# A hybrid encoder layer on one core: convolution bias on VectorE, group-norm statistics per pass, another order of the last four output pieces

## The chip, the cores and the metric

The kernel runs on one core of one Trainium2 chip. A core has a matrix engine (TensorE, PE in the profile; PEld is its weight load), VectorE (DVE), ScalarE (ACT), GpSimd (POOL) and SyncE (SP), which here issues every DMA. Matrix products land in PSUM, everything else lies in SBUF. The metric is the device time of one execution in microseconds. Of the kernel before there are three timed runs: 1142.69 us in the middle, 1141.70 and 1143.29 at the ends. The profile comes from one more execution, of 1140.08 us.

## What is computed

One layer with batch 1, 1024 positions and width 1024. Its first half mixes tokens: a normalised and modulated input goes through one projection, whose columns are split between a convolution group (512 channels) and an HGRN2 group of four heads; both results go through one output projection. The second half is an MLP of width 4096 with a squared ReLU. All in float32. The part that the change touches, cut down:

```python
def _conv_mixer(u_val, u_gate, w_dw, b_dw, gn_gain, gn_bias):
    u = u_val * jax.nn.sigmoid(u_gate)
    y = causal_depthwise_conv(u, w_dw) + b_dw          # 31 taps, 512 channels
    yf = y.reshape(B, S, CONV_GROUPS, CONV_CH // CONV_GROUPS)   # 8 groups of 64 channels
    mu = jnp.mean(yf, axis=-1, keepdims=True)
    var = jnp.mean(jnp.square(yf - mu), axis=-1, keepdims=True)
    yf = ((yf - mu) * lax.rsqrt(var + GN_EPS)).reshape(B, S, CONV_CH)
    return jax.nn.silu(yf * gn_gain + gn_bias)
```

`u_val` and `u_gate` come from the combined projection. Mean and variance are taken at each position over the 64 channels of a group.

## The kernel before

Matrix products are made with float32 operands split into a high and a low part: three matmuls for each product. ACT makes the high part, and DVE or POOL the low part (`split`, `halve`); which of the two is decided when the program is built.

The order of all instructions on all engines is fixed when the program is built. The class `Weave` keeps an estimated time for each engine and a list of side streams (Python generators). The main stream issues the big matmuls; at each of its steps the side streams whose due time has come issue their next piece. A changed cost, or a stream added at another moment, therefore moves instructions of other streams too. On the chip each engine takes its instructions strictly in that order and waits where an operand isn't there.

Stages, with their times on the profile's clock: the first three projections (to 73 us); gate, value and V columns (G, U, V, to about 257); the convolution between the last V columns and the following projections (232 to 296); the remaining projections `pj` beside the four HGRN2 heads (to 378); the output projection `pout` (to about 510); the MLP's up part `pup` (to 823); its down part, which alternates between the PSUM tiles `al` and `be` (to 1132).

**Convolution.** The gated input `u` is written to a DRAM buffer `udram`, and read back as `wide`, so that a window of 64 rows, 32 of a block of positions and 32 of the block before, lies in 64 partitions. `toep` holds Toeplitz matrices of the taps: a window's row times this matrix gives 32 outputs of one channel. The 512 channels go in two passes `p`, each with two rounds `q` of 64 channels times two partition halves `r`. Each pass loads `toep` (4 tiles), then `wide` by four DMAs, two for each half `r`. Row 0 of each window meets no tap (31 taps over 32 outputs leave it unused), so the host put the bias `b_dw` in row 0 of the Toeplitz matrices, and two more DMAs (line 710) overwrite row 0 of each half of `wide` with ones. SP issues such a DMA only when the load of the same half has landed, and what stands behind it in SP's order waits too.

The matmuls of a round write the PSUM tile `cv` (one buffer). `conv_evac` copies it on ACT into four result tiles `ys[s]`, 256 positions each, by 8 copies of 128 elements a round; the copies scatter (a step of 128 elements in the destination). When the last round of the second pass is copied, four streams `conv_norm(s)` start: DVE takes the mean over 64 channels for 16 groups (`gmu`, 128x16), subtracts it, ACT squares the whole tile, DVE sums the squares (`gvar`), POOL raises to the power -1/2 (`gr`), DVE multiplies. Then PE transposes the tile (`cpb`), ACT applies gain and bias, and a sigmoid and a product follow; the result is one operand of the output projection.

**Heads.** Each head takes q and f from projections `pj`. A matmul with ones (`pd`) and seven levels of small matmuls (`pl`, with block size h = 1 to 64) build its attention. Each level is a chain: `pl` on PE needs the q and k that DVE scaled for the level before.

**Last pieces.** The last down product `p4` has four output pieces `al[0]` to `al[3]` (128x512). `al[0]` and `al[1]` are halves of one PSUM tile, `al[2]` and `al[3]` of another. For the last three groups of the sum the main stream takes piece after piece, 18 matmuls each. After each piece a stream `last(n)` reads it on ACT (squares) and DVE (product with the gate), makes the norm's factor on POOL, adds to the residual on DVE and stores. A matmul that writes a PSUM tile waits until the readers of that tile are done.

Of the kernel before, what the change touches and what calls it, by code (L numbers as in the profile page):

```python
# [7 lines left out]
F32 = mybir.dt.float32  # L8
# [3 lines left out]
AF = mybir.ActivationFunctionType  # L12
ALU = mybir.AluOpType
AX = mybir.AxisListType

P = 128
# [34 lines left out]
EARLY, LATE = (4, 5, 0, 1, 2, 3), (6, 7)  # L51
FINAL = (0, 1, 3, 2, 5, 6, 4, 7)
# [155 lines left out]
class Weave:  # L208
# [30 lines left out]
    def after(self, key, extra=None):  # L239
        return max(self.t[key], self.now) + (EXTRA if extra is None else extra)  # L240
# [47 lines left out]
def block_kernel(ctx: ExitStack, tc: tile.TileContext, x, vecs, masks, rows, vrow, crow, wada_t, wada_n,  # L288
                 win0, win, wint, toep, wout, wup, wdn, out):
# [25 lines left out]
    def tiny(name, cols=1):  # L315
        if cols > 8:
            return small.tile([P, 16], F32, tag="tiny16", name=name, bufs=8)[:, 0:cols]
        return small.tile([P, 8], F32, tag="tiny", name=name, bufs=16)[:, 0:cols]
# [342 lines left out]
    S.dma_start(crow_s.f, crow.broadcast_to([P, 1024]))  # L661
    sig = [None] * 4
# [34 lines left out]
    def conv_input():  # L697
        yield slots.gone
        w = slots.wide().rearrange("p (b c) -> p b c", c=P)
        for p in range(2):  # L700
            yield room(4)
            toeps = [new() for _ in range(4)]
            for c in range(4):
                S.dma_start(toeps[c].f, toep[p, c])
            for r in range(2):
                nc.sync.dma_start(w[64 * r:64 * r + CB, :, :], udram[2 * p + r, :, 0:NB, :])
                nc.sync.dma_start(w[64 * r + CB:64 * r + 64, :, :], udram[2 * p + r, :, 1:NB + 1, :])
                wv.spend("S", 5.0)
            for r in range(2):
                nc.sync.dma_start(w[64 * r:64 * r + 1, :, :], ones[0:CB, :])  # L710
            yield wv.t["S"] + 2 * DLAT
            yield from conv_mm(p, w, toeps)
        slots.end_wide()
# [22 lines left out]
    def conv_evac(p, q, ps):  # L736
        pv = ps.rearrange("p (r i b) -> p r i b", r=2, i=16)
        for s in range(4):
            if ys[s] is None:
                yield room(1)  # L740
                ys[s] = new()
            yv = ys[s].f.rearrange("t (b p r q i) -> t p q r i b", p=2, r=2, q=2, i=16)
            for r in range(2):
                A.activation(yv[:, p, q, r], pv[:, r, :, 8 * s:8 * s + 8], AF.Copy)
        acc.done(ps, "A")
        yield after("A")
        if p and q:
            for s in range(4):
                wv.add(conv_norm(s), RNORM)

    def conv_norm(s):

        y = ys[s]
        yield after("A")
        yv = y.f.rearrange("p (a c) -> p a c", c=64)
        mu = tiny("gmu", 16)
        V.reduce_sum(mu, yv, axis=AX.X)
        V.tensor_scalar(mu, mu, 1.0 / 64, None, ALU.mult)
        V.tensor_tensor(yv, yv, mu[:, :, None].broadcast_to([P, 16, 64]), ALU.subtract)
# [3 lines left out]
        A.activation(sz.f, y.f, AF.Square)  # L763
        yield after("A")
        var = tiny("gvar", 16)
        V.reduce_sum(var, sz.f.rearrange("p (a c) -> p a c", c=64), axis=AX.X)
        r = rstd_of(var, 16, 1.0 / 64, 1e-5, "gr")
        yield after("G")
        V.tensor_tensor(yv, yv, r[:, :, None].broadcast_to([P, 16, 64]), ALU.mult)
        yield after("V")  # L770
# [985 lines left out]
    def down():  # L1756
# [32 lines left out]
        for n in range(4):  # L1789
            yield from down_mm("p4", al, False, range(NG - LASTG, NG), (n,))  # L1790
            wv.add(last(n, al[n]), -1)
# [89 lines left out]
def host_arrays(np, i):  # L1881
# [9 lines left out]
    for h in MASKED:  # L1891
# [18 lines left out]
    taps[0] = f("b_dw")[0]  # L1910
# [6 lines left out]
                win0=win0, win=win, wint=wint, toep=toep, wout=wo, wup=wup, wdn=wdn)  # L1917
# [18 lines left out]
```

## Time and profile before

| | us |
|---|---|
| median of three timed runs | 1142.69 (1141.70 to 1143.29) |
| the profiled execution | 1140.08 |
| its span, first to last instruction | 1138.3 |
| mean granted TensorE clock (share of full speed) | 0.979 |
| POOL busy | 282.2 |
| matmuls | 7036 |

A line of a timeline gives the start, the duration, engine, source line, operation, output and inputs, shapes and the number of instructions merged; in brackets stands how long the engine had been idle and what ended that. A line of a table of stretches gives busy time and number of instructions for PE, PEld, DVE, ACT and POOL in turn, then the granted clock, the share of the DMA engines and GB/s. A line of a group gives count, total busy time and mean in ns, then idle time before it. L235 is the helper that records the instructions of DVE, ACT, POOL and most DMAs, L1820 that of the matmuls, L413 the power of a norm. `s` stands for any of the 53 large SBUF tiles.

### The profile page before, as it was taken

Reading aid. Unit: us, or ns where it says so; the run is one execution under the profiler, and the core shown is the slowest. Engines: PE = TensorE matmul, PEld = TensorE weight load, DVE = VectorE, ACT = ScalarE, POOL = GpSimd, SP = SyncE. Lnnn points to the kernel's source line nnn. Section 1 sums busy time; section 2 is a strip of 40 time slices with the busy share of each in tenths; the row PEclk is TensorE's granted clock in tenths of the full one; section 3 lists DMA queues with packets and bytes.
Section 4 is the critical chain, followed back from the end, with each engine's and each line's share of the span. In section 5 each row is a group of like instructions: output and inputs, shape, how many; then the busy total and the mean of one; then the engine's idle time right before and its main releaser. Section 6 shows DMA issues by size and latency. Waiting matters only on the chain.

```text
span 1138.3 us, 17072 instructions
## 1 busy us (share of the span) xinstructions
PE 1089.6 (96%) x7036; PEld 886.2 (78%) x7036; DVE 708.1 (62%) x727; ACT 471.1 (41%) x687; POOL 282.2 (25%) x190
## 2 busy tenths in 40 slices
PE   6999989889999799989999999999999999999996
PEld 2787778768878688767888888888888888888885
DVE  3537667234588962665766975333266969997942
ACT  6731301014356423567452243556543334454530
POOL 5121131001193400482101420124400002304301
PEclk8999999989999799989999999999999999999999
DMA  9523434756021202374569745325667957674901
GB/s 365 198 73 127 147 105 136 198 165 176 23 75 56 94 2 56 113 261 169 197 244 324 290 166 194 112 56 170 218 237 268 326 203 245 217 278 153 336 11 74
DMA packets 57149, 195.21 MB, mean 171 GB/s; under 512 B 6256, under 2 KB 10736, under 8 KB 56816
## 3 DMA queue, kind: packets, MB, share of 16 engines
q1 hardware_dynamic: 57072, 194.13, 49.6%
q8 instruction: 55, 0.90, 0.3%
q14 instruction: 22, 0.18, 0.0%
HBM read 158.32 MB, written 35.72 MB: 170 GB/s over the span
## 4 chain that ended last, share of the span: by engine, by line
PE 78%; DVE 8%; DMA 7%; issue 2%; POOL 2%; ACT 2%; SPq 1%; DVEq 0%; POOLq 0%; ACTq 0%
PE pup L1820 26%; PE al L1820 15%; PE be L1820 11%; PE pout L1820 8%; DVE s L235 7%; PE pj L1820 6%; PE pf L1820 3%; DMA s<-in_wada_n 2%; PE ptV L1820 2%; POOL s L235 1%; ACT s L235 1%; PE po L1820 1%; PE cv L1820 1%; DMA wide<-udram 1%; PE pt L1824 1%
## 5 line engine op out<-in xcount | busy, mean ns | idle before, releaser
L235 DVE TENSOR_TENSOR s<-s,s 128x1024 fp32r<-128x1024 f32 (+3 forms) x342 | 419.5, 1263 | 95.7 <-ACT s L235 65.9
L235 ACT ACTIVATE s<-s 128x1024 fp32r<-128x1024 f32 (+2 forms) x317 | 304.0, 993 | 361.6 <-DVE s L235 198.9
L235 POOL TENSOR_TENSOR s<-s,s 128x1024 fp32r<-128x1024 f32 (+4 forms) x83 | 188.0, 2272 | 555.5 <-ACT s L235 468.1
L1820 PE MATMUL pup<-s,s 128*128 128x512 f32 x1344 | 308.1, 390 | 0.0
L1820 PEld LDWEIGHTS pup<-s,s 128*128 128x128 f32 x1344 | 251.5, 188 | 51.9
L1820 PE MATMUL al<-s,s 128*128 128x512 f32 x768 | 175.6, 390 | 3.1 <-DVE s L235 3.1
L1820 PEld LDWEIGHTS al<-s,s 128*128 128x128 f32 x768 | 143.9, 188 | 34.2 <-DVE s L235 4.3
L1820 PE MATMUL be<-s,s 128*128 128x512 f32 x576 | 131.0, 389 | 0.0
L1820 PEld LDWEIGHTS be<-s,s 128*128 128x128 f32 x576 | 108.1, 188 | 22.5
L1820 PE MATMUL pj<-s,s 128*128 128x512 f32 x432 | 108.2, 401 | 2.2 <-POOL s L235 2.2
L1820 PE MATMUL pout<-s,s 128*128 128x512 f32 x384 | 100.9, 416 | 4.6 <-DVE s L235 4.1
L1820 PEld LDWEIGHTS pj<-s,s 128*128 128x128 f32 x432 | 80.2, 191 | 19.1 <-POOL s L235 2.7
L1820 PEld LDWEIGHTS pout<-s,s 128*128 128x128 f32 x384 | 74.4, 200 | 20.8 <-DVE s L235 4.6
L235 DVE SCALAR_TENSOR_TENSOR s<-s,c_act,s 128x1024 f32<-128x1024 f32 x28 | 40.6, 1449 | 52.7 <-DMA s<-in_wada_n 52.4
L235 DVE TENSOR_TENSOR s<-pup,s 128x1024 f32<-128x1024 f32 x24 | 29.3, 1222 | 46.8 <-PE pup L1820 46.6
L235 DVE SCALAR_TENSOR_TENSOR s<-pup,s 128x1024 f32<-128x1024 f32 x16 | 19.6, 1225 | 53.3 <-PE pup L1820 50.3
L1820 PE MATMUL ptU<-s,s 128*128 128x512 f32 x192 | 47.3, 400 | 0.0
L1820 PE MATMUL ptV<-s,s 128*128 128x512 f32 x192 | 46.2, 400 | 0.0
L1820 PE MATMUL ptG<-s,s 128*128 128x512 f32 x192 | 45.9, 394 | 0.0
L413 POOL TENSOR_TENSOR ors<-ors,mhalf 128x4 f32<-128x4 f32 x8 | 10.0, 1259 | 144.7 <-DVE ors L235 144.6
L235 ACT ACTIVATE junk<-s 128x1024 bf16<-128x1024 f32 (+1 forms) x30 | 29.9, 998 | 31.0 <-DVE s L235 23.8
L1820 PEld LDWEIGHTS ptV<-s,s 128*128 128x128 f32 x192 | 36.5, 192 | 7.8
(125 smaller groups left out, 815.6 us busy)
## 6 DMA issues: line engine op xcount, KB each, us to landing
s<-in_wdn SPq DMA_DIRECT2D x72, 512.0 KB
s<-in_wup SPq DMA_DIRECT2D x56, 512.0 KB
s<-in_wada_n SPq DMA_DIRECT2D x32, 512.0 KB
s<-in_x SPq DMA_DIRECT2D x16, 512.0 KB
s<-in_wada_t SPq DMA_DIRECT2D x16, 512.0 KB
u<-s SPq DMA_DIRECT2D x16, 512.0 KB
s<-u SPq DMA_DIRECT2D x16, 512.0 KB
s<-in_wint SPq DMA_DIRECT2D x12, 512.0 KB
```

Of the source, the lines that this page charges most:

```text
L235: return op(*a, **k)
L413: nc.gpsimd.tensor_tensor(r, r, mhalf[:, 0:n], ALU.pow)
L1820: return self.te.matmul(out, lhsT=lhsT, rhs=rhs, **k)
L1824: return self.te.transpose(out, in_, identity)
```

## The change

Four things. The rows of ones and the bias in the Toeplitz matrices go. A new input `cbias` (128x128, 64 KB) is loaded once, the same in all partitions, and `conv_evac` adds it while it moves `cv` out of PSUM, on DVE instead of ACT, with 4 instructions of 256 elements a round instead of 8 of 128. The statistics of the group norm are taken after each pass, over that pass's half of the channels (8 groups a tile, `conv_stats`), and only the rest waits for the second pass (`conv_out`). The last four output pieces are made in the order 0, 2, 1, 3. Beside these the ring of small 8-column tiles has 12 buffers instead of 16.

```diff
+LAST = (0, 2, 1, 3)
...
-        return small.tile([P, 8], F32, tag="tiny", name=name, bufs=16)[:, 0:cols]
+        return small.tile([P, 8], F32, tag="tiny", name=name, bufs=12)[:, 0:cols]
...
+    cb = const.tile([P, P], F32, name="cb")
+    S.dma_start(cb, cbias)
...
-            for r in range(2):
-                nc.sync.dma_start(w[64 * r:64 * r + 1, :, :], ones[0:CB, :])
...
     def conv_evac(p, q, ps):
         pv = ps.rearrange("p (r i b) -> p r i b", r=2, i=16)
+        bias = cb.rearrange("p (a r q i) -> p a q r i", a=2, r=2, q=2)[:, p, q]
...
-            for r in range(2):
-                A.activation(yv[:, p, q, r], pv[:, r, :, 8 * s:8 * s + 8], AF.Copy)
-        acc.done(ps, "A")
-        yield after("A")
-        if p and q:
+            V.tensor_tensor(yv[:, p, q], pv[:, :, :, 8 * s:8 * s + 8],
+                            bias[:, :, :, None].broadcast_to([P, 2, 16, 8]), ALU.add)
+        acc.done(ps, "V")
+        yield after("V", 0)
+        if q:
             for s in range(4):
-                wv.add(conv_norm(s), RNORM)
-
-    def conv_norm(s):
+                wv.add(conv_stats(p, s), RNORM)
+
+    def conv_stats(p, s):
 
         y = ys[s]
-        yield after("A")
-        yv = y.f.rearrange("p (a c) -> p a c", c=64)
-        mu = tiny("gmu", 16)
+        yv = y.f.rearrange("p (b a c) -> p a b c", a=2, c=64)[:, p]
+        mu = tiny("gmu", 8)
         V.reduce_sum(mu, yv, axis=AX.X)
         V.tensor_scalar(mu, mu, 1.0 / 64, None, ALU.mult)
-        V.tensor_tensor(yv, yv, mu[:, :, None].broadcast_to([P, 16, 64]), ALU.subtract)
+        V.tensor_tensor(yv, yv, mu[:, :, None].broadcast_to([P, 8, 64]), ALU.subtract)
+        yield after("V")
+        sq = half512("gsq")
+        sv = sq.rearrange("p (b c) -> p b c", c=64)
+        A.activation(sv, yv, AF.Square)
+        yield after("A")
+        var = tiny("gvar", 8)
+        V.reduce_sum(var, sv, axis=AX.X)
+        r = rstd_of(var, 8, 1.0 / 64, 1e-5, "gr")
+        yield after("G")
+        V.tensor_tensor(yv, yv, r[:, :, None].broadcast_to([P, 8, 64]), ALU.mult)
+        if p:
+            wv.add(conv_out(s), RNORM)
...
-        for n in range(4):
+        for n in LAST:
             yield from down_mm("p4", al, False, range(NG - LASTG, NG), (n,))
             wv.add(last(n, al[n]), -1)
...
-    taps[0] = f("b_dw")[0]
+    cbias = f("b_dw")[0].reshape(2, 4, 64).transpose(1, 0, 2).reshape(4, 1, P).repeat(CB, 1).reshape(P, P)
```

How the change moves instructions is seen in the built programs' order.

SP's queue at the first pass of the convolution. `in_toep` are Toeplitz tiles, `wide<-udram` the windows, two loads for each half; `in_wada_n` feeds the modulation, `in_win` a later projection. Before:

```order
L235 DMA s_1750<-in_toep 128x1024
L706 DMA wide<-udram 32x4096
L707 DMA wide<-udram 32x4096
L710 DMA wide<-ones 1x32x128 x2
L235 DMA s_245<-in_wada_n 128x1024
L235 DMA s_773<-in_win 128x1024
```

And now:

```order
L236 DMA s_1752<-in_toep 128x1024
L709 DMA wide<-udram 32x4096
L710 DMA wide<-udram 32x4096
L236 DMA s_245<-in_wada_n 128x1024
L236 DMA s_775<-in_win 128x1024
```

(The pair of loads is shown once; there are two, one for each half.) The two DMAs of ones are gone, and the next loads stand directly behind the windows.

POOL's queue around the norm. `gr` is the norm's power, `ors` that of a head's output, `mfull` a head's output on its way to the output projection, `s_526` and `s_600` are low parts of projection weights. Before:

```order
L235 TENSOR_TENSOR s_2625<-mfull,s_2624 128x512
L235 TENSOR_SCALAR s_2921<-s_2921,omlb,lb 128x1024
L235 TENSOR_SCALAR s_2922<-s_2921 128x1024
L413 TENSOR_TENSOR gr<-gr,mhalf 128x16
L235 TENSOR_TENSOR s_2715<-mfull,s_2714 128x512
L235 TENSOR_TENSOR s_526<-s_773,s_525 128x1024
L413 TENSOR_TENSOR gr<-gr,mhalf 128x16 x3
L235 TENSOR_TENSOR s_600<-s_773,s_599 128x1024
```

And now:

```order
L414 TENSOR_TENSOR gr<-gr,mhalf 128x8 x4
L236 TENSOR_TENSOR s_526<-s_775,s_525 128x1024
L414 TENSOR_TENSOR ors<-ors,mhalf 128x4 x2
L236 TENSOR_TENSOR s_2805<-mfull,s_2804 128x512
L414 TENSOR_TENSOR ors<-ors,mhalf 128x4 x2
L414 TENSOR_TENSOR gr<-gr,mhalf 128x8 x4
L236 TENSOR_TENSOR s_2722<-mfull,s_2721 128x512
L236 TENSOR_TENSOR s_2805<-mfull,s_2804 128x512
L236 TENSOR_SCALAR s_2993<-s_2993,omlb,lb 128x1024
```

The powers now stand in two groups of four, one for each pass. The weight split that stood between the powers (`s_526`, for the fourth projection behind the convolution) is no longer in POOL's queue at this place; it is in DVE's. (The `s_526` split shown now is that of an earlier projection.)

PE's order at the fourth level of head 2 (`pl`, 32x16), with the projections `pj` and the output projection `pout` around it. Before:

```order
L1820 MATMUL pj_3356<-s_114,s_599 128x512 x2
L1820 MATMUL pj_3356<-s_113,s_600 128x512 x2
L1820 MATMUL pl<-s_3023,s_2922 32x16 x32
L1820 MATMUL pout<-s_3353,s_2624 128x512 x2
L1820 MATMUL pout<-s_3354,s_2624 128x512 x2
```

And now:

```order
L1829 MATMUL pj_3299<-s_112,s_525 128x512 x2
L1829 MATMUL pj_3299<-s_111,s_526 128x512 x2
L1829 MATMUL pl<-s_3124,s_2994 32x16 x32
L1829 MATMUL pj_3299<-s_113,s_525 128x512 x2
L1829 MATMUL pj_3299<-s_114,s_525 128x512 x2
```

The level stood behind the last projection; now it stands within the last but one, and the levels behind it stand in the last projection, 18 projection matmuls apart.

PE's order at the first change of piece at the end, with buffer numbers, since the tiles are told apart by them. Before:

```order
L1820 MATMUL al_6800<-s5_8805,s36_8806 128x512
L1820 MATMUL al_6800<-s27_8804,s30_8807 128x512
L1820 MATMUL al_6800<-s52_8730,s32_8732 128x512
L1820 MATMUL al_6800<-s18_8731,s32_8732 128x512
L1820 MATMUL al_6800<-s52_8730,s17_8733 128x512
```

And now:

```order
L1829 MATMUL al_6834<-s5_8839,s27_8840 128x512
L1829 MATMUL al_6834<-s32_8838,s4_8841 128x512
L1829 MATMUL al_6835<-s33_8764,s38_8766 128x512
L1829 MATMUL al_6835<-s28_8765,s38_8766 128x512
L1829 MATMUL al_6835<-s33_8764,s12_8767 128x512
```

Before, the second piece lies in the same PSUM tile as the first; now in the other.

More of the change, by code (lines that the diff above doesn't have):

```diff
@@ L288, in block_kernel @@
 def block_kernel(ctx: ExitStack, tc: tile.TileContext, x, vecs, masks, rows, vrow, crow, wada_t, wada_n,
-                 win0, win, wint, toep, wout, wup, wdn, out):
+                 win0, win, wint, toep, cbias, wout, wup, wdn, out):
     nc = tc.nc
@@ L742, in conv_evac, with conv_out @@
             yv = ys[s].f.rearrange("t (b p r q i) -> t p q r i b", p=2, r=2, q=2, i=16)
-            for r in range(2):
-                A.activation(yv[:, p, q, r], pv[:, r, :, 8 * s:8 * s + 8], AF.Copy)
-        acc.done(ps, "A")
-        yield after("A")
-        if p and q:
+            V.tensor_tensor(yv[:, p, q], pv[:, :, :, 8 * s:8 * s + 8],
[3 more added lines that the diff above has]
+        if q:
             for s in range(4):
-                wv.add(conv_norm(s), RNORM)
-    def conv_norm(s):
+                wv.add(conv_stats(p, s), RNORM)
+    def conv_stats(p, s):
         y = ys[s]
-        yield after("A")
-        yv = y.f.rearrange("p (a c) -> p a c", c=64)
-        mu = tiny("gmu", 16)
+        yv = y.f.rearrange("p (b a c) -> p a b c", a=2, c=64)[:, p]
+        mu = tiny("gmu", 8)
         V.reduce_sum(mu, yv, axis=AX.X)
         V.tensor_scalar(mu, mu, 1.0 / 64, None, ALU.mult)
-        V.tensor_tensor(yv, yv, mu[:, :, None].broadcast_to([P, 16, 64]), ALU.subtract)
+        V.tensor_tensor(yv, yv, mu[:, :, None].broadcast_to([P, 8, 64]), ALU.subtract)
[11 more added lines that the diff above has]
+            wv.add(conv_out(s), RNORM)
+    def conv_out(s):
+        y = ys[s]
         yield after("V")
@@ L762, in conv_norm @@
         sz, z = new(), new()
[L763 to L770, printed above, removed]
         for h in range(2):
@@ L1916, in host_arrays @@
     arrs = dict(x=f("x")[0], vecs=vecs, masks=masks, rows=rows, vrow=b_in[None, 2048:2560], crow=crow, wada_t=wada_t, wada_n=wada_n,
-                win0=win0, win=win, wint=wint, toep=toep, wout=wo, wup=wup, wdn=wdn)
+                win0=win0, win=win, wint=wint, toep=toep, cbias=cbias, wout=wo, wup=wup, wdn=wdn)
     return {k: np.ascontiguousarray(v) for k, v in arrs.items()}
```

## The prediction

> **What bounds the kernel now.** I read the page first: the engines' shares, then the chain that ended last.
>
> ```profile
> PE 1089.6 (96%) x7036; PEld 886.2 (78%) x7036; DVE 708.1 (62%) x727; ACT 471.1 (41%) x687; POOL 282.2 (25%) x190
> PE 78%; DVE 8%; DMA 7%; issue 2%; POOL 2%; ACT 2%; SPq 1%; DVEq 0%; POOLq 0%; ACTq 0%
> ```
>
> PE is the bound: 1089.6 of 1138.3 us busy. The change removes no matmul, so it can only touch the 48.7 us in which PE waits and the stretches in which its clock is halved. The list of waits of PE names them (total, times, longest):
>
> ```profile
> PE pl L1820 <- DVE s L235: 11.2, 6, 3.5
> PE cv L1820 <- DMA wide<-ones: 7.4, 1, 7.4
> PE pout L1820 <- DVE s L235: 4.1, 2, 3.6
> PE al L1820 <- DVE s L235: 3.1, 2, 1.6
> PE pj L1820 <- POOL s L235: 2.2, 1, 2.2
> ```
>
> All five lie near the edits: the rows of ones (cv), the four last pieces (al), the norm and its neighbours (pj, pl, pout).
>
> **The last four pieces.** From the timeline of the end:
>
> ```profile
> 1116.77 0.60 ACT L235 ACTIVATE junk<-al 128x512 bf16<-128x512 f32 x1 [23.97 <-PE al L1820]
> 1117.49 0.69 DVE L235 SCALAR_TENSOR_TENSOR s<-al,s 128x512 f32<-128x512 f32 x1 [21.27 <-ACT junk L235]
> 1118.23 8.47 PE L1820 MATMUL al<-s,s 128*128 128x512 f32 x36 [1.56 <-DVE s L235]
> 1128.27 3.71 PE L1820 MATMUL al<-s,s 128*128 128x512 f32 x15 [1.56 <-DVE s L235]
> ```
>
> Pieces 0 and 1 share one PSUM tile, 2 and 3 the other. Piece 1 waits 1.56 us until ACT and DVE have read piece 0; then 36 matmuls (pieces 1 and 2) run without a break, since 2 has the other tile; piece 3 waits again. In the order 0, 2, 1, 3 every neighbour lies in the other tile, and a tile is read (1.4 us) while 18 matmuls of the other run (4 us). What follows the last matmul is unchanged. Gain 2 x 1.56 = **3.1 us**; nothing covers it and nothing else becomes late, as the stores only come 1.5 us closer together.
>
> **The rows of ones.** The DMA issues and PE around the first convolution:
>
> ```profile
> 224.36 0.62 SPq L710 DMA_DIRECT2D wide<-ones  x1
> 229.22 0.55 SPq L710 DMA_DIRECT2D wide<-ones  x1
> 229.86 0.53 SPq L235 DMA_DIRECT2D s<-in_wada_n  x1
> 232.04 1.74 PE L1820 MATMUL cv<-wide,s 64*32 64x32 f32 x128 [7.45 <-DMA wide<-ones]
> 233.71 2.93 PE L1820 MATMUL ptV<-s,s 128*128 128x512 f32 x6
> ```
>
> The 7.45 us isn't all the ones'. Each of the two ones DMAs waits for the load of the half that it overwrites, so their issue times date the landings: 224.36 and 229.22. Without ones PE waits for the second half itself, to 229.2: gain 232.04 - 229.22 = **2.8 us**, not 7.4. The wait left is 4.6 us, so the half clock behind it (six ptV in 2.93 us, where six at the full clock's 0.226, worked out below, are 1.4) mostly stays; with it gone another 1.5 us would come. SP no longer stands behind the ones: the loads of 229.86 are issued right behind the udram loads, ahead of nothing PE needs earlier, if the transfers keep their order (third rival if not). In the second pass PE had other work until its cv at 275.35, so there I take zero. The 64 KB load of the bias stands in SP's queue at 62 us, where SP is idle from 63.0 to 77.84: hidden, 0.4 us of issue without that cover.
>
> ```profile
> 62.64 0.38 SPq L235 DMA_DIRECT2D udram<-s  x1
> 77.84 0.33 SPq L235 DMA_DIRECT2D s<-in_win  x1
> ```
>
> **Bias and statistics.** Groups kept apart by form (total, mean ns):
>
> ```profile
> L235 ACT ACTIVATE s<-cv 128x128 f32<-128x128 f32 x32 | 8.2, 435 | 13.9 <-PE ptV L1820 5.9 <-PE cv L1820 5.8 <-DMA s<-in_wada_n 2.1
> L235 DVE TENSOR_TENSOR s<-ptV,vbias 128x256 f32<-128x256 f32 x16 | 5.7, 417 | 11.1 <-PE ptV L1820 11.1
> L235 DVE TENSOR_REDUCE gmu<-s 128x16 f32<-128x1024 f32 x4 | 4.8, 1212 | 0.0
> L235 DVE TENSOR_TENSOR s<-s,gmu 128x1024 f32<-128x1024 f32 x4 | 4.9, 1225 | 0.2
> L235 DVE TENSOR_TENSOR s<-pg,s 128x512 f32<-128x512 f32 x4 | 2.7, 683 | 2.1 <-PE pg L1820 2.1
> L413 POOL TENSOR_TENSOR gr<-gr,mhalf 128x16 f32<-128x16 f32 x4 | 12.2, 3076 | 0.1
> L413 POOL TENSOR_TENSOR ors<-ors,mhalf 128x4 f32<-128x4 f32 x8 | 10.0, 1259 | 144.7 <-DVE ors L235 144.6
> ```
>
> ACT loses 32 copies (8.2 us) and squares eight halves instead of four wholes. DVE gains 16 bias adds of 256 elements from PSUM. The nearest row, an add of that size from PSUM, gives 0.42 each, 6.7 us; at the ACT copy's rate per element (435 ns for 128, the same scattered writes) 0.87 each, 13.9. I take 0.42. The norm's 16 wide DVE operations of about 1.22 become 32 of 512 elements, at 0.68 by the row of that size: 19.5 becomes 21.8 us. POOL's powers are 8 of 128x8 for 4 of 128x16: between 1.3 (the 128x4 row) and 3.1 each, I take 1.5, half of the 128x16. Half of all this now runs at 252 to 272 us, where DVE is a third busy (21.2 of 63 us):
>
> ```profile
> 237.00:300.00 63.00, 62.42 (x1154) 52.98 (x1143) 21.20 (x38) 22.46 (x83) 4.08 (x3) 1.00 0.47 133
> 300.00:400.00 100.00, 91.70 (x663) 73.44 (x662) 88.98 (x92) 49.49 (x82) 52.49 (x23) 0.91 0.21 69
> ```
>
> What it costs there: the adds of the first PSUM tile are done about when ACT's copies were (both wait for a slot that ptV frees), and DVE has finished the first pass's norm by 271.5, counted from the cv's end at 251.7 with 6 us for the means and 1.5 per power; PE wants the pS results among it at 272 to 274. Cost taken as zero, cover about 1 us. In the next stretch DVE is the full engine, 89.0 of 100 us, and loses 20 - 11 - 3 = 6 us of work (half the norm out, eight adds in).
>
> There PE lost, in time and clock:
>
> ```profile
> 318.13 2.90 POOL L413 TENSOR_TENSOR gr<-gr,mhalf 128x16 f32<-128x16 f32 x1
> 322.25 3.40 POOL L235 TENSOR_TENSOR s<-s,s 128x1024 fp32r<-128x1024 f32 x1
> 325.70 6.40 PE L1820 MATMUL pj<-s,s 128*128 128x512 f32 x20 [2.25 <-POOL s L235]
> ```
> ```profile
> 380.72 1.05 PE L1820 MATMUL pl<-s,s 128*32 128x16 f32 x64 [3.45 <-DVE s L235]
> 381.71 2.93 PE L1820 MATMUL pout<-s,s 128*128 128x512 f32 x6
> 384.44 1.05 PE L1820 MATMUL pd<-s,ones_r 128*128 128x512 f32 x2
> 387.60 0.73 PE L1820 MATMUL pl<-s,s 128*16 128x16 f32 x64 [2.11 <-DVE s L235]
> 388.83 2.92 PE L1820 MATMUL pout<-s,s 128*128 128x512 f32 x6 [0.49 <-DVE s L235]
> ```
> ```profile
> 325.70:332.00 6.30, 6.30 (x21) 5.04 (x22) 5.79 (x6) 0.00 (x0) 6.30 (x2) 0.73 0.54 168
> 381.60:394.00 12.40, 9.79 (x99) 7.30 (x92) 11.40 (x19) 4.14 (x7) 3.85 (x2) 0.50 0.38 134
> 524.00:1084.00 560.00, 560.00 (x2482) 463.34 (x2481) 381.38 (x291) 254.04 (x256) 122.16 (x53) 1.00 0.63 219
> ```
>
> The last row gives 560/2482 = 0.226 us a matmul at full clock. Waits: 2.25 + 3.45 + 2.11 + 0.49 = 8.3 us. Half clock: 20 pj in 6.40 against 4.5 us, 1.9 lost; 18 pout and 4 pd between 381.7 and 394.6 in 9.5 against 5.0, 4.5 lost. Together 14.7 us.
>
> The first wait was a weight split that stood in POOL behind a power of the norm. In the new order that split is DVE's, behind no power: its ACT half comes at 318.5 and PE wants it at 325. The norm ends near 312 (it ended at 338.4), so head 2's q and k come out of DVE sooner and its levels (pl) stand among the projections, 18 matmuls (4.1 us) apart, each asking DVE for 3.2 to 3.5 us. Walking the new order with these durations, DVE is ahead of PE at the five levels of head 2 behind the first by 4, 5, 6, 6 and 2.6 us, but only 0.8 us ahead at head 3's first. Beside POOL, DVE's two-input work stretches:
>
> ```profile
> 334.92 5.75 POOL L235 TENSOR_TENSOR s<-s,s 128x1024 fp32r<-128x1024 f32 x2
> 334.99 3.42 DVE L235 TENSOR_TENSOR s<-s,gr 128x1024 f32<-128x1024 f32 x1 [1.63 <-POOL gr L413]
> ```
>
> 3.42 for 1.22 us, 2.2 more a collision. So I leave one new wait of 2.0 us with one half-clock stretch of 1.9: 14.7 - 3.9 = **10.8 us**.
>
> The Trainium skill's page "SBUF — State Buffer" (section "SBUF: two separate sides") has it that a VectorE operation with two SBUF inputs and a GpSimd operation shut each other out for the whole instruction. That speaks against the change, which makes more such subtractions and products; the pair above agrees in kind, and by it alone, with a collision for each of the 16 of them, up to 35 us of DVE time would be added, mostly off PE's path.
>
> The page "TensorE: Matmul & The Clock Gate" ("Why this matters for your kernels") asks only for no idle gaps of more than about 3 us. Here 2.25 us of waiting was followed by a granted clock of 0.73, so the trace is harsher; by the page the 1.9 us term falls away and the sum is 1.9 us smaller.
>
> **Sum.** 3.1 + 2.8 + 10.8 = 16.7 us. The profiled execution took 1140.08 us (span 1138.3), so 1123.4; the median of the runs shown is 1142.69, 2.6 above, and for a median I predict **1126.0**.
>
> **Rivals.**
> 1. The pl waits stay. DVE was 89% busy and POOL's splits still collide with it; only the pj wait goes. 3.1 + 2.8 + 2.25 + 1.9 = 10.0 us, 1132.7. Against it: the 6 us taken off DVE and the wider spacing. 0.12.
> 2. Every middle wait finds a successor (ACT's evacuations of cpb, now denser, or a split in POOL): 5.9 us, 1136.8. For it: in the same walk ACT has under 0.5 us to spare at two cpb. 0.12.
> 3. The two loads that SP now issues at once (1 MB) share the engines with the udram loads: at the 210 GB/s seen at 232 to 237 us that is 5.0 us, cv starts at 234.2, term two is -2.2, total 11.7, 1131.0. Against it: the two halves landed 4.9 us apart, in order of issue. 0.07.
> 4. **Slower.** Operations of 512 elements don't halve: the 32 stay at 1.22 in place of 0.68, 17 us more on DVE, first at 252 to 272 us, where PE's pS and po wait with 1 us of cover. With two half-clock stretches 21 us against 16.7: 1147. It decides from about 1.1 us an operation; the pg row (0.68) speaks against it. 0.05.
> 5. The change doesn't do what it says (the last pieces still wait for a shared tile): together with losses elsewhere no change, 0.04.
>
> **Numbers.** Forecast 0.60, from 1120 (all 14.7 and the 1.5 of the clock: 21.1 us, rounded) to 1131. The range 1120 to 1138 takes in rivals 1 to 3 with their spread, and leaves out 4, 5 and the far end of 2. Two tenths of a per cent, 2.3 us, is about what a measurement of this kernel can tell from no change: faster 0.89, the same 0.06, slower 0.05.
>
> **What would show it.** Right: two waits of al gone; cv waiting for wide<-udram, about 4.6 us; no wait of pj near 325; norm's last product before 315; waits of pl after 350 under 3 us. Wrong: bias adds over 0.9 us, a cv wait of over 7 us, pS or po waiting for DVE near 270, or a clock below 0.8 in 360 to 400.

## The result, and the profile after

| us | before | after |
|---|---|---|
| median, first set of runs (5 and 5) | 1141.70 | 1134.17 (1133.72 to 1137.44) |
| ratio, with its 95% interval | | 0.9941 [0.9923, 0.9959] |
| median, a second set (13 and 6) | 1142.36 | 1136.11 (1132.65 to 1137.24) |
| ratio, second set | | 0.9941 [0.9918, 0.9964] |
| the profiled execution | 1140.08 | 1134.17 |
| its span | 1138.3 | 1132.1 |
| mean granted clock | 0.979 | 0.983 |

The change makes the kernel 0.6% faster: 5.9 us between the profiled executions, 6.7 by the ratio. The forecast was 16.7. The direction was right and the time lies in the range, but the gain is about two fifths of the sum at most.

The page of after: the engines' shares, and the chain that ended last.

```profile
PE 1085.9 (96%) x7036; PEld 883.8 (78%) x7036; DVE 715.4 (63%) x764; ACT 464.1 (41%) x659; POOL 292.3 (26%) x197
PE 77%; DVE 8%; DMA 7%; ACT 2%; issue 2%; POOL 1%; SPq 1%; DVEq 0%; POOLq 0%; ACTq 0%
```

The matmuls are the same 7036. DVE took 7 us more and ACT 7 us less, as the edits say; POOL took 10 us *more*, which no term of the sum had. The waits of PE in after (total, times, longest):

```profile
PE cv L1829 <- DMA wide<-udram: 8.2, 2, 5.4
PE pout L1829 <- DVE s L236: 7.3, 3, 3.7
PE pl L1829 <- DVE s L236: 6.5, 5, 3.2
PE tn L1833 <- DVE s L236: 2.6, 1, 2.6
PE pj L1829 <- issue: 1.1, 1, 1.1
```

Beside the list of before: `al` is gone (3.1), `pj`'s wait for POOL is gone (2.2), `pl` fell from 11.2 to 6.5. But `pout` rose from 4.1 to 7.3, `tn` (PE's transposes of a head's keys) is new with 2.6, and `cv`, which had waited 7.4 for the ones, now waits 8.2 for the windows themselves. So three things are to be explained: the tail, which came as forecast; the convolution's start, which came later and not earlier; and the middle, where new waits stand for the old.

The middle is best read from two fixed points of PE: the start of `cv` in earnest (the first matmul behind which the others follow without another wait for data) and the start of `pout`'s long run of over 100 matmuls. The starts of single executions scatter by 2 us before `cv`; the distance takes that out, though it scatters too: two kernels below whose instructions are the same up to the end of the middle (statistics only, and statistics and tail) differ by 2.3 us. These are the numbers of every kernel in this text:

| kernel | cv in earnest | pout's run | between | ratio to before, interval |
|---|---|---|---|---|
| before | 232.04 | 463.96 | 231.9 | |
| after | 233.17 | 461.49 | 228.3 | 0.9941 [0.9923, 0.9959] |
| after, second set | 235.35 | 463.58 | 228.2 | 0.9941 [0.9918, 0.9964] |
| after, SP held | 231.62 | 461.55 | 229.9 | 0.9933 [0.9912, 0.9954] |
| after, four dates | 231.17 | 460.02 | 228.9 | (no interval) |
| after, one-input operations on POOL | 233.56 | 456.43 | 222.9 | 0.9909 [0.9889, 0.9930] |
| after, six splits on DVE | 233.24 | 455.76 | 222.5 | 0.9899 [0.9880, 0.9918] |
| after, two splits on DVE | 235.28 | 461.31 | 226.0 | 0.9917 [0.9900, 0.9933] |
| after, SP held, six splits on DVE | 230.86 | 453.90 | 223.0 | 0.9871 [0.9848, 0.9895] |
| after, all 18 splits on DVE | 231.63 | 453.41 | 221.8 | 0.9856 [0.9832, 0.9880] |
| after, SP held, all 18 splits on DVE | 229.17 | 450.46 | 221.3 | 0.9868 [0.9842, 0.9893] |
| before, four splits on DVE | 233.12 | 466.38 | 233.3 | 0.9980 [0.9967, 0.9994] |
| before, tail only | 232.13 | 464.36 | 232.2 | 0.9965 [0.9948, 0.9981] |
| before, bias only | 234.12 | 466.57 | 232.5 | 0.9992 [0.9978, 1.0006] |
| before, statistics only | 232.45 | 460.61 | 228.2 | 0.9943 [0.9924, 0.9962] |
| before, statistics and tail | 232.75 | 458.60 | 225.9 | 0.9915 [0.9894, 0.9935] |

From before to after `cv` starts 1.1 us later, the middle is 3.6 us shorter, and the tail 3.1: together 5.6 of the 5.9 us.

The middle as a row, between its two fixed points, in before, in after and with the statistics alone (PE, PEld, DVE, ACT, POOL, clock, DMA share, GB/s):

```profile
232.04:463.96 231.92, 222.18 (x2599) 182.85 (x2599) 137.46 (x188) 95.70 (x235) 63.01 (x31) 0.95 0.26 78
233.17:461.49 228.32, 219.35 (x2596) 180.35 (x2596) 145.12 (x225) 88.43 (x207) 72.40 (x38) 0.98 0.25 76
232.45:460.61 228.16, 218.25 (x2598) 179.19 (x2599) 140.09 (x214) 97.18 (x239) 64.18 (x33) 0.98 0.26 80
```

PE idles 9.7 us of the middle in before and 9.0 in after. So of the 3.6 us only 0.8 are idle time; 2.8 are the same matmuls in less busy time, at a higher granted clock (0.95 and 0.98). The old waits are gone, but nearly as much new waiting stands in their place.

### The profile page after: what moved, and what is told of

It reads as the page before. It is cut to its first block, busy times and chain, and to the rows that moved or that the text cites. A ratio compares the mean times of both kernels' runs of the same rounds, so it can differ in the third digit from the quotient of the medians.

```text
span 1132.1 us, 17081 instructions
## 1 busy us (share of the span) xinstructions
PE 1085.9 (96%) x7036; PEld 883.8 (78%) x7036; DVE 715.4 (63%) x764; ACT 464.1 (41%) x659; POOL 292.3 (26%) x197
## 4 chain that ended last, share of the span: by engine, by line
PE 77%; DVE 8%; DMA 7%; ACT 2%; issue 2%; POOL 1%; SPq 1%; DVEq 0%; POOLq 0%; ACTq 0%
PE pup L1829 26%; PE al L1829 15%; PE be L1829 12%; DVE s L236 8%; PE pout L1829 7%; PE pj L1829 6%; PE pf L1829 3%; DMA s<-in_wada_n 2%; ACT s L236 2%; PE ptV L1829 2%; DMA wide<-udram 2%; PE po L1829 1%; PE cv L1829 1%; PE pt L1833 1%; POOL s L236 1%
## 5 line engine op out<-in xcount | busy, mean ns | idle before, releaser
L236 DVE TENSOR_TENSOR s<-s,s 128x1024 fp32r<-128x1024 f32 (+3 forms) x340 | 415.1, 1258 | 108.8 <-ACT s L236 70.5
L236 ACT ACTIVATE s<-s 128x1024 fp32r<-128x1024 f32 (+2 forms) x313 | 300.6, 992 | 354.2 <-DVE s L236 202.6
L236 POOL TENSOR_TENSOR s<-s,s 128x1024 fp32r<-128x1024 f32 (+4 forms) x85 | 195.1, 2304 | 558.8 <-ACT s L236 457.8
L1829 PEld LDWEIGHTS ptU<-s,s 128*128 128x128 f32 x192 | 36.3, 192 | 7.9
```

The source lines that it names most:

```text
L236: return op(*a, **k)
L1829: return self.te.matmul(out, lhsT=lhsT, rhs=rhs, **k)
```

## The experiments

### The convolution's start: held, and dated

In after SP issues the loads of `in_wada_n` and `in_win` right behind the windows. The timeline of SP and of PE:

```profile
212.92 0.43 SPq L709 DMA_DIRECT2D wide<-udram  x1
...
215.45 0.42 SPq L710 DMA_DIRECT2D wide<-udram  x1
216.16 0.35 SPq L236 DMA_DIRECT2D s<-in_wada_n  x1
217.44 0.35 SPq L236 DMA_DIRECT2D s<-in_win  x1
```
```profile
227.48 0.28 PE L1829 MATMUL cv<-wide,s 64*32 64x32 f32 x2 [2.78 <-DMA wide<-udram]
233.17 1.55 PE L1829 MATMUL cv<-wide,s 64*32 64x32 f32 x126 [5.42 <-DMA wide<-udram]
```

Two matmuls of the first half run at 227.48, and the rest when the second half has landed, at 233.17, not at the 229.2 of the forecast. **SP held** puts one small DMA behind the windows:

```diff
+            if p == 0:
+                nc.sync.dma_start(hold, w[95:97, NB - 1, :])
```

> The kernel after, with one more DMA of 1 KB on SP behind the four window loads of the first pass: it reads two rows of the last load (two partitions, 128 elements each) and so holds SP, and with it the loads of in_wada_n and in_win, until the second half has landed; PE does not wait for it. Theory (the two loads issued at once share the DMA engines with the windows): the first half lands at about 224.4 us and the second at about 229.2 as before the change, not 227.4 and 233.1; cv begins in earnest at about 229.3, not 233.17; in_wada_n is used at about 234, as now; the time falls by 3 to 4 us against the kernel after (about 1130.5). Rival (the windows land late for another reason, such as the transfers of u before them): the second half lands within 1 us of 233, and the time stays within 1 us. Second rival (the head start is lost again in the middle, where DVE sets the pace): cv begins 3.9 us earlier, but pout's long run at 461.66 moves by under 1.5 us.

Measured: 1133.92 us (1130.11 to 1135.47), ratio 0.9933 [0.9912, 0.9954], as fast as after within the intervals. SP and PE of this kernel:

```profile
231.54 0.23 SPq L714 DMA_DIRECT2D hold<-wide  x1
231.87 0.36 SPq L236 DMA_DIRECT2D s<-in_wada_n  x1
```
```profile
227.12 0.27 PE L1832 MATMUL cv<-wide,s 64*32 64x32 f32 x2 [2.06 <-DMA wide<-udram]
231.62 1.55 PE L1832 MATMUL cv<-wide,s 64*32 64x32 f32 x126 [4.23 <-DMA wide<-udram]
```

`cv` came 1.6 us earlier, less than half of what my theory gave, and the first half landed at 227.1 as in after, not at 224.4. So the early loads explain a part; the dates themselves had to be wrong. The second rival's case came as well: `pout`'s run starts at 461.55, and at 461.49 in after, so the head start was lost again on the way. **Four dates** lets SP issue one DMA for each load:

```diff
+            if p == 0:
+                for i in range(4):
+                    nc.sync.dma_start(hold[i:i + 1, :], w[32 * i:32 * i + 1, NB - 1, :])
```

> The kernel after, with four small DMAs (512 B each) on SP behind the four window loads of the first pass; each reads a row that only one of the loads writes, so SP issues it when that load has landed, and its issue time dates the landing. Theory (the four loads land one by one, and the rows of ones of the kernel before lay in the first and the third alone, so that their issue at 224.36 and 229.22 dated these two and not the halves): issues at about 224.4, 227.1, 229.2 and 231.6 us, cv in earnest at 231.6. Rival (both loads of a half land together, and the earlier issue of the ones before the change had another cause): pairs at about 227.1 and 231.6.

SP's timeline, issue by issue, and PE's behind it (one execution, of 1132.31 us):

```profile
224.48 0.22 SPq L715 DMA_DIRECT2D hold<-wide  x1
226.80 0.21 SPq L715 DMA_DIRECT2D hold<-wide  x1
229.33 0.21 SPq L715 DMA_DIRECT2D hold<-wide  x1
231.05 0.21 SPq L715 DMA_DIRECT2D hold<-wide  x1
```
```profile
231.17 1.57 PE L1833 MATMUL cv<-wide,s 64*32 64x32 f32 x126 [4.03 <-DMA wide<-udram]
```

The theory's case came: the four loads land one behind another, about 2.2 us apart. The first and third lie 4.85 us apart, as the two issues of ones in before (224.36 and 229.22, 4.86 apart): row 0 of a half lies in the first of its two loads, so the ones never dated the halves. The last load landed at 231.05, and PE started 0.1 us behind it. The rows of ones had cost 0.9 us beside that (232.04 against 231.17). By the averages of the five profiles with ones, 232.5, and the four in which SP was held, 230.7, it is 1.8; counted in each profile from the third load's landing, 2.5 on average of the five and 1.8 here, it is 0.7. The two early loads cost about 1.5 us: between the two matmuls of the first half and the rest lie 5.3 to 6.0 us in the seven profiles with early loads, 5.6 on average, and 3.7 to 4.5 in the four without, 4.1 on average.

### Where the middle's new waits come from

The stretch of the new waits in after: PE's timeline, then DVE's and POOL's (the longest operations one by one), and the stretch as a row:

```profile
382.68 1.20 PE L1829 MATMUL pout<-s,s 128*128 128x512 f32 x4 [1.54 <-DVE s L236]
386.90 2.65 PE L1829 MATMUL pout<-s,s 128*128 128x512 f32 x6 [2.09 <-DVE s L236]
397.02 0.71 PE L1833 MATMUL tn<-msk,s 128*128 128x128 f32 x4 [2.59 <-DVE s L236]
397.43 4.79 PE L1829 MATMUL pout<-s,s 128*128 128x512 f32 x13
```
```profile
374.77 4.45 DVE L236 TENSOR_TENSOR s<-s,s 128x512 f32<-128x512 f32 x2 [0.93 <-PE pl L1829]
379.14 2.35 DVE L236 TENSOR_TENSOR s<-s 128x16 f32<-128x16 f32 x1
...
385.57 1.27 DVE L236 SCALAR_TENSOR_TENSOR s<-pj,vec,s 128x1024 f32<-128x1024 f32 x1
...
388.01 2.18 DVE L236 TENSOR_TENSOR s<-s,s 128x512 f32<-128x512 f32 x1
390.11 2.87 DVE L236 TENSOR_TENSOR s<-s,s 128x512 f32<-128x512 f32 x1
392.91 2.85 DVE L236 TENSOR_TENSOR s<-s 128x512 f32<-128x512 f32 x1
```
```profile
374.32 7.13 POOL L236 TENSOR_TENSOR s<-s,s 128x1024 fp32r<-128x1024 f32 x3 [1.17 <-ACT s L236]
387.26 2.38 POOL L236 TENSOR_TENSOR s<-s,s 128x1024 fp32r<-128x1024 f32 x1 [5.81 <-ACT s L236]
389.60 2.83 POOL L236 TENSOR_TENSOR s<-s,s 128x1024 fp32r<-128x1024 f32 x1
392.40 2.81 POOL L236 TENSOR_TENSOR s<-s,s 128x1024 fp32r<-128x1024 f32 x1
```
```profile
374.00:400.00 26.00, 19.43 (x175) 14.97 (x175) 25.19 (x23) 13.14 (x20) 15.62 (x7) 0.89 0.31 103
```

DVE's last three operations, about 0.65 us each when alone (below), end at 390.19, 392.98 and 395.76; POOL's end at 389.64, 392.43 and 395.21. Each of DVE's ends 0.55 us behind one of POOL's: it stands until POOL is through. `tn` waits behind these three. The longer wait of `pout` ends when DVE has read the last projection's PSUM tile (385.57 + 1.27 = 386.84), and that read stands behind an earlier group: three of POOL's subtractions from 374.32 to 381.45, and DVE's pair of products and a small operation (2.35 us; 0.18 with POOL's third subtraction taken out, below) beside them. DVE is busy for 25.2 of 26 us here, but much of that is standing. The three later POOL operations, and the third of the earlier group, are low parts of output weights; the new order dealt six of these eight subtractions to POOL, the order of before four. **One-input operations on POOL** takes the second input of these six away, and leaves their low parts out (they become zero):

```diff
+                nc.gpsimd.tensor_scalar(lo, hi.bitcast(F32), 0.0, 0.0, ALU.mult, ALU.add)
+                nc.gpsimd.tensor_scalar(lo, src, 0.0, 0.0, ALU.mult, ALU.add)
```

> The kernel after, in which POOL makes the low parts of six output weights (in_wout) with two one-input operations each, times zero, in place of one subtraction of two tiles: the low parts of these weights are left out, the order of all other instructions stays, and POOL stays busy about as long. Theory (POOL's two-input subtractions stretch DVE's two-input operations, and this makes the new waits of pout and tn): in 374 to 400 us DVE's 512-element products fall from 1.54 us to about 0.7 each, 11 us of stretch in all disappear; PE's waits there (6.6 us: pout 3.6, tn 2.6, pl 0.3) fall under 2.5; the time falls by 4 to 6 us against the kernel after. Rival (the output weights or DVE's own queue are late by themselves): DVE may be faster, but PE still waits 5 us or more there and the time stays within 1.5 us. Third possibility (any POOL operation stretches DVE): DVE's products stay over 1.2 us.

**Six splits on DVE** has in the same place:

```diff
+                nc.vector.tensor_tensor(lo, src, hi.bitcast(F32), ALU.subtract)
```

> The kernel after, in which the same six subtractions stand in DVE's queue in place of POOL's, at the places where their turn comes; the order on PE, ACT and SP is unchanged. DVE gains 6 x 1.22 = 7.3 us of work and loses the 11 us of stretch. Theory (collisions): PE's waits in 374 to 400 us fall by 2 to 4 us and the time by 2 to 5 us. Rival (a split in DVE's queue waits for its weight, which lands late, and holds the levels behind it): waits of 5 us or more, no gain or up to 4 us slower.

Measured: 1130.47 us (1128.19 to 1133.82) for the first and 1129.14 (1127.71 to 1130.73) for the second, 3.7 and 5.0 below after. The groups of DVE in 374 to 400 us, in after, with one-input operations, and with the six on DVE:

```profile
L236 DVE TENSOR_TENSOR s<-s,s 128x512 f32<-128x512 f32 x8 | 12.0, 1542 | 0.9 <-PE pl L1829 0.9
L236 DVE TENSOR_TENSOR s<-s 128x512 f32<-128x512 f32 x1 | 2.9, 2853 | 0.0
L236 DVE TENSOR_TENSOR s<-s 128x16 f32<-128x16 f32 x1 | 2.4, 2353 | 0.0
```
```profile
L236 DVE TENSOR_TENSOR s<-s,s 128x512 f32<-128x512 f32 x10 | 11.9, 1228 | 3.8 <-PE pl L1834 3.8
```
```profile
L236 DVE TENSOR_TENSOR s<-s,s 128x512 f32<-128x512 f32 x10 | 9.6, 1000 | 2.7 <-PE pl L1833 2.7
L354 DVE TENSOR_TENSOR s<-s,s 128x1024 fp32r<-128x1024 f32 x4 | 4.9, 1226 | 0.0
```

And with the six on DVE the stretch as a row, PE's remaining wait, and DVE before its end:

```profile
374.00:400.00 26.00, 22.79 (x240) 18.02 (x235) 23.92 (x31) 12.96 (x18) 4.01 (x2) 0.93 0.33 103
```
```profile
385.28 2.69 PE L1833 MATMUL pout<-s,s 128*128 128x512 f32 x6 [2.88 <-DVE s L236]
```
```profile
383.95 1.27 DVE L236 SCALAR_TENSOR_TENSOR s<-pj,vec,s 128x1024 f32<-128x1024 f32 x1
```

DVE gained four subtractions of 1.23 us in this stretch and yet was busy for less time, and PE's idle time fell from 6.6 to 3.2 us; the middle shrank from 228.3 to 222.5. The weights' arrival is not what limits: the wait that is left ends when DVE has read the last projection's PSUM tile (383.95 + 1.27 = 385.22, PE goes on at 385.28). The theory's cause holds: the time falls by 3.7 us when only POOL's second inputs go, and by 5.0 when the six operations leave POOL. Two of its figures for the first kernel do not: I had expected 0.7 us for the products, and they took 1.23 on average, and 4 to 6 us of gain, and it was 3.7. A first pair at 374 us still meets two two-input operations of POOL that are no output weights, and the one-input operations hold DVE back too, the third possibility that I had named (at the end of this text).

Which of POOL's six? **Two splits on DVE** moves only k = 2 and 3, which were DVE's before the change:

```diff
-        yield from split(st.f, hi.r, lo.r)
+        yield from split(st.f, hi.r, lo.r, k in (2, 3))
```

> The kernel after, in which only the low parts of the fifth and sixth output weight (k = 2 and 3) are made on DVE, as in the kernel before; the other four stay on POOL, as they were before the change too. All other instructions keep their order. With all six on DVE the time fell by 5.0 us and PE's waits in 374 to 400 us from 6.6 to 3.2. Theory A (the two splits that the change moved to POOL made the new waits): at least half of that comes back, 2.5 to 5 us. Theory B (it is the four that were POOL's in the kernel before too, which now hit the levels of head 3): under 1.5 us.

1131.60 us (1130.96 to 1133.42), 2.6 below after and 2.5 above the six. The wait of `tn` is gone, the two of `pout` stay (3.6). So by the medians half of the loss is the two splits that the change moved, just over theory A's bound, and the other half the four that POOL always had; the interval of this kernel overlaps those of its two neighbours, so the halves are not exact. Did these cost the kernel before as much? **Before, four splits on DVE** is the same edit there.

> The kernel before, in which the four subtractions of output weights that stood on POOL are on DVE, in the same order otherwise. Theory (the waits of pl of the kernel before at 377 to 389 us, 3.45, 2.11 and 0.49, and the half clock behind them, come from the same collisions): 3 to 6 us faster than the kernel before. Rival (they come from DVE's load with the norm, as the prediction had it): under 1.5 us.

1138.47 us (1137.00 to 1143.03), ratio 0.9980 [0.9967, 0.9994]: 2.3 us by the ratio, between theory and rival. Its profiled execution still waits 5.8 us for `pl`, 4.4 of it at once, and its middle is no shorter (233.3). The waits of before were mostly not these collisions. Whether the same four subtractions cost more since the change is not shown: by the times it is 2.3 us before and 2.5 after, by the middle nothing before and 3.5 us after (226.0 against 222.5).

### The parts of the change alone

**Tail only** is the kernel before with the new order of pieces, **bias only** has the bias on DVE and no ones, **statistics only** takes the statistics per pass with ones and copies as before.

```diff
-        for n in range(4):
+        for n in (0, 2, 1, 3):
...
-        if q:
+        if p and q:
             for s in range(4):
-                wv.add(conv_stats(p, s), RNORM)
+                wv.add(conv_norm(s), RNORM)
...
+            for r in range(2):
+                A.activation(yv[:, p, q, r], pv[:, r, :, 8 * s:8 * s + 8], AF.Copy)
-            V.tensor_tensor(yv[:, p, q], pv[:, :, :, 8 * s:8 * s + 8],
-                            bias[:, :, :, None].broadcast_to([P, 2, 16, 8]), ALU.add)
```

(The first piece against before; the second is bias only and the third statistics only, both against after.)

> The kernel before, with the last four output pieces in the order 0, 2, 1, 3 and nothing else changed. Theory: the two waits of al of 1.56 us go and nothing takes their place, 3.1 us less than the kernel before (ratio 0.9973), nothing else moves. Rival (the second pair's readers, now closer together, delay the last store): 1.6 us or less.

1137.29 us (1133.81 to 1140.44), 4.0 us below before by the ratio, whose interval (2.2 to 5.9) holds the 3.1. PE has no wait of `al` in its profile.

> The kernel before, with the bias added on DVE and the rows of ones gone, and nothing else: statistics as before in one piece behind the second pass, last pieces in the old order, 16 small buffers. Theory (the middle's gain comes from the statistics being taken per pass): cv in earnest at about 233.2 us as in the kernel after, 1.1 later than before, and the time within 1.5 us of the kernel before. Rival (it comes from the bias part, which takes 32 copies off ACT and moves the order of POOL's splits): 3 us or more faster, with pout's long run of 114 at or before 461 us in place of 463.96.

1140.86 us (1137.54 to 1144.08), no difference that can be measured. `cv` at 234.12, the middle at 232.5: the theory's side.

> The kernel before, with the statistics taken per pass and nothing else: rows of ones, the bias in the Toeplitz matrices and the copies on ACT stay, the last pieces keep the old order, 16 small buffers. The bias part alone moved the time by under 0.1%. Theory (the middle's gain is that of the statistics per pass alone): cv at 232 us as before, no wait of pj for POOL near 325, the time 2.5 to 6 us below the kernel before. Rival (the gain needs both parts, since each alone deals the splits out anew between POOL and DVE; here five of the eight output weights' subtractions stand on POOL): within 1.5 us of the kernel before.

1135.64 us (1134.76 to 1139.04), 6.5 us below before by the ratio. `cv` stays at 232.45 (two matmuls; the rest follow at 233.26, behind 0.5 us in which PE waited for nothing that the profile shows), and the middle is 228.2 us, as long as in after. So, as far as single profiles tell, the statistics carry the whole gain of the middle; and, as in after, it is a gain in clock (0.98) and not in idle time (9.9 us). Added up, tail, bias and statistics give more (4.0 + 0.9 + 6.5 us by ratios) than the whole change (6.7). The change **without its bias part** is statistics only and tail only together:

> The kernel before with the statistics per pass and the last pieces in the order 0, 2, 1, 3, that is the change without its bias part (rows of ones, bias in the Toeplitz matrices and copies on ACT stay). Measured apart: statistics 0.9943, tail 0.9965, bias part 0.9992, the whole 0.9941. Theory A (the parts add, and the bias part costs time when it stands with the others, by the two early loads and the splits that move to POOL): about 0.991, 1131.5 to 1133. Theory B (statistics 3.8 us by the trace and tail 3.1 add to 6.9, the rest is the spread of the runs, and the bias part costs 1 us at most): about 0.994, 1134.5 to 1136.

1131.86 us (1130.31 to 1133.75), ratio 0.9915 [0.9894, 0.9935]: theory A's side, 3 us below after. The interval overlaps that of after by 0.001, so the bias part costs the change likely, not certainly, some 3 us. Two causes are seen in traces: `cv` starts at 233.8 on average of the seven profiles with early loads, and at 232.5 in the five with ones; and here five of the output weights' subtractions stand on POOL, not six. How much each counts is not shown. That the middle is 225.9 us here and 228.2 in the kernel with the same work up to that point shows how much one profile scatters.

### Versions that beat both

**After, SP held and six splits on DVE** has the two edits shown above together:

> The kernel after with both edits: SP held until the fourth window load has landed, and the six subtractions of output weights on DVE. Held alone, cv came 1.5 us earlier and the time stayed, which I put down to the collisions in 374 to 400 us. Theory (with these gone the head start lasts): 1 to 2 us below the version with the subtractions alone (1129.1), so about 1127.6. Rival (something else in the middle sets the pace, such as the later in_wada_n): within 0.5 us of it, or above.

1127.20 us (1125.70 to 1130.50), 1.9 below the version without the hold, though the intervals overlap; `cv` and `pout`'s run are 2.4 and 1.9 us earlier. **All 18 splits on DVE** has, in `split` itself:

```diff
-            G.tensor_tensor(lo, src, hi.bitcast(F32), ALU.subtract)
+            nc.vector.tensor_tensor(lo, src, hi.bitcast(F32), ALU.subtract)
+            wv.spend("G", 0.55 + n / 520)
```

(The second line keeps the planner's account of POOL, and so the order of everything else.)

> The kernel after, with all 18 subtractions of `split` that stood on POOL in DVE's queue (the six of the output weights among them), in the same order otherwise. Theory (POOL's other two-input subtractions stretch DVE as well, in 262 to 374 us): 1 to 3 us below the version with the six alone (1129.1). Rival (outside 374 to 400 us DVE is ahead of PE, so its stretch costs nothing, and a split that waits for its weight now holds DVE's queue): within 1 us of it, or up to 4 us slower.

1125.90 us (1123.95 to 1127.31), 3.2 below the version with the six alone: the theory's side. The change itself was measured again beside these:

> The kernel after, unchanged, on the same chip as the other three, so that they can be compared with it directly: 1132.5 to 1135.5 us.

1136.11 us (1132.65 to 1137.24), a little above what I had expected; the 18 splits are 10.2 us below it. In 374 to 400 us PE idles 2.1 us with them. And **SP held with all 18 splits on DVE:**

> The kernel after with SP held until the fourth window load has landed and all 18 subtractions of `split` on DVE. Theory (both gains last): cv in earnest about 1.5 us earlier than without the hold, and 1 to 1.5 us below the version without it (1125.9): about 1124.6, the fastest of all. Rival (DVE sets the pace behind 262 us): within 0.5 us of 1125.9.

1126.05 us (1123.61 to 1127.22). The trace shows the head start kept (`cv` 2.5 us and `pout`'s run 3.0 us earlier), the times don't, which is the rival's case: whether the hold is worth anything beside the other edit stays open.

## Why the prediction was wrong, and where it was right

The sum was 3.1 for the tail, 2.8 for the rows of ones and 10.8 for the middle; the profiles show 3.1, −1.1 and 3.6. That the time lies in the range is not to the sum's credit: two of its three terms failed, and the range was wide enough for the second and third rival. (The gain behind the lower bound of the range, "21.1 us", is 22.1 by its own terms, 3.1 + 2.8 + 14.7 + 1.5.)

**The tail, 3.1 us: right.** Both waits of `al` are gone, nothing took their place, and alone it gives this within its interval.

**The rows of ones, 2.8 us: wrong, −1.1.** The step that failed is "their issue times date the landings: 224.36 and 229.22". A DMA of ones waits for the one load that writes row 0, not for the half ("the load of the same half", in the words on the kernel before, is the first of its two); the load that PE needed last came 1.7 us after it (229.33, 231.05). The sentence on the order of transfers failed too: the two loads that SP now issues at once pushed the second half of the windows back by about 1.5 us (the runs show the delay; that it comes from sharing the DMA engines is argued). That is the third rival, to which I gave 0.07, since the landings "4.9 us apart, in order of issue" spoke against it; but these dates belonged to two loads of the four, and the order of issue says nothing on what a later load takes away. Its price, 5.0 us, was too high. Nor would an earlier `cv` have reached the end by itself, as the sum took it to do: with SP held it came 1.6 us earlier, and the time stayed.

**Bias and statistics, cost zero: about right for the operations themselves.** The 16 adds took 0.62 us each by the mean of their group and 8.2 us in all (0.42 and 6.7 forecast), the operations of 512 elements 0.67 to 0.69 beside 0.68 (the products with the power 0.83, since one met POOL and took 1.78), the powers 1.8 beside 1.5. The fourth rival fell with that. Neither `pS` nor `po` waited for DVE near 270. What the bias part likely costs beside that, some 3 us, was not in the sum.

**The middle, 10.8 us: wrong in size, 3.6.** The old waits went as the steps had it: no wait of `pj` for POOL near 325, the norm's last product begun at 313.69, under 1 us of `pl` behind 350, a clock of 0.93 in 360 to 400; so the first rival fell too. The term that was mis-sized is the "one new wait of 2.0 us with one half-clock stretch of 1.9". There were four waits in 374 to 400 us, 6.6 us in all, with two stretches of lower clock behind them (below), and 2.4 us of smaller ones elsewhere in the middle; PE's idle time fell by 0.8 us in place of the 6.3 that the sum has (8.3 less 2.0). The walk that gave DVE's lead took DVE's products at the durations that they have alone; the prediction had seen a collision (3.42 for 1.22 us) and allowed for a single wait from it, though the order put six subtractions on POOL beside the last head's levels. With POOL's six subtractions moved to DVE (four of them were POOL's before too) the middle is 222.5, 9.4 us shorter than before. By its size the outcome is the second rival's, 5.9 us, and "Every middle wait finds a successor" is nearly what happened; the size agrees by luck, as the rows of ones gave −1.1 and not the 2.8 that this rival keeps. The rival's cause, ACT's evacuations or a split in POOL that PE waits for, is not what happened: the split was in time, and it was DVE that stood.

By the Trainium skill's page "SBUF — State Buffer" ("SBUF: two separate sides") a two-input operation of VectorE and a GpSimd operation shut each other out for the whole instruction. The trace agrees: the three products above, each through only when POOL's instruction was. The prediction put this rule's price "mostly off PE's path", looking at the norm; it lay on the path, at the output weights.

A lower clock followed waits of about 2 us again: six `pout` in 2.65 us behind 2.09, thirteen in 4.79 behind 2.59, where six and thirteen at 0.226 are 1.4 and 2.9.

## What to carry to other kernels

A DMA that waits for data dates only the load that writes the bytes it touches; where the time of a whole transfer matters, date its last piece. When a change frees an engine's queue, ask what that queue will now issue earlier and beside which transfer, and when a planner deals work out anew, price each of POOL's two-input operations at the time it takes from DVE in the stretch where DVE sets PE's pace. Here all 18 such splits on DVE were worth more than the change itself (10.2 us beside 6.7). And count PE's idle time before and after, not only the waits that are gone: here the old ones went and the idle time stayed.

## What the runs showed of the hardware that I had not expected

POOL's one-input operations hold DVE back as well, only for less. DVE's pair of products at the first level of the last head, with two-input operations on POOL, with one-input ones, and with none:

```profile
388.01 4.98 DVE L236 TENSOR_TENSOR s<-s,s 128x512 f32<-128x512 f32 x2
```
```profile
387.03 2.69 DVE L236 TENSOR_TENSOR s<-s,s 128x512 f32<-128x512 f32 x2
```
```profile
387.51 1.29 DVE L236 TENSOR_TENSOR s<-s,s 128x512 f32<-128x512 f32 x2
```

4.98, 2.69 and 1.29 us for the same two products. Beside the one-input operations DVE's two products and the one that follows end at 388.28, 389.72 and 391.18, again 0.53 to 0.55 us behind three operations of POOL (at 387.75, 389.18 and 390.63). The smaller loss fits their length, 1.05 to 1.41 us here and 2.38 to 2.83 with two inputs. In the same profile a pair of products at a time when POOL is idle takes what it takes with none:

```profile
393.51 1.30 DVE L236 TENSOR_TENSOR s<-s,s 128x512 f32<-128x512 f32 x2 [1.10 <-PE pl L1834]
```
